# The samples' memory updates of an mLSTM layer in four row tiles, with selection products to lay out their rows, and one accumulator shared between the weight stream and the mixers

## The chip, the cores and the metric

One Trainium2 chip; the program runs on one core. The metric is the device time of one launch in microseconds, the median of several runs.

## The reference

Two layers run over 288 tokens: 256 of a prompt and 8 samples of 4 tokens. Layer 0 has an S5 and a GLA mixer, layer 1 an mLSTM with 4 heads of width 512; each layer ends in an MLP with squared ReLU. For this case the mLSTM's update of the samples' memories matters. Each of 8 samples has for each of 4 heads a memory of 512x512 that is read against q, decayed, given the products of its 4 tokens, and returned:

```python
num = jnp.einsum('bhts,bhse->bhte', sc, vc) + wp[..., None] * jnp.einsum('bhtd,bhde->bhte', qc, cm)
...
c_new = decay[..., None, None] * cm + jnp.einsum('bhs,bhsd,bhse->bhde', wk, kc, vc)
```

All of it is float32.

## The kernel before

**The stream.** Almost all work is products of the 288 tokens with weight matrices. `gemm` cuts a matrix into groups of 256 output columns, and each group into granules of 4 k-tiles. For a granule, SyncE loads the weights (`raw`), ScalarE rounds them to `wh` and VectorE forms the rest `wl` (`cast`, L187 and L188), and `mm` issues 2 x 4 x 3 = 24 matmuls of 128x128 by 288 columns (L202 to L204) into the group's two accumulators, PSUM tiles named `g` of the pool `psg`, which has 3 buffers. The group's last granule is followed by the evacuation of the two accumulators, mostly on VectorE. In layer 1 a group of the input projections has 4 granules, one of the output product 2.

**The side work.** The mixers are generators. After each granule `run` casts weights for a later granule and then lets every active generator advance (`pump`); a rate says how many steps it takes per granule. So the program's order on each engine is fixed when it is built: 24 stream matmuls, then whatever the generators issue in that step, then the next 24. TensorE works through this in order. PSUM has 8 banks: `psg` 3, `pss` 3 (tiles `s`, for nearly all side work), `psn` 2 (tiles `n`). The tiles of a pool are given out in turn, and a new tile waits until the last reader of the tile that held its buffer is done.

**The mLSTM.** `ml_head` prepares a head: the products of the prompt and the rows of k and v for the samples. A sample's k and v are split into a rounded part and a rest, and the four combinations stand in 128 rows (`ks0`, `vs`). `ml_mem` updates the memories. They come in 64 tiles `cin` of two samples (128x2x512) by GpSimd's DMA queue, 6 buffers. The function `masked` makes, once for four tiles, stationary operands `km` with all rows but one sample's set to zero. A step (rate 0.64) takes one tile; every second step first reads two tiles against q in four column tiles of 32 columns (L1545, tiles `n`):

```python
for b in range(2):
    pb = self.pss.tile([128, 512], F32, name="s")
    nc.tensor.matmul(pb, lhsT=km[:, 2 * i + b, :], rhs=vs, start=True, stop=True)
    c = 4 * (2 * i + b) + 3
    v.scalar_tensor_tensor(out=t[:, b, :], in0=t[:, b, :], scalar=wp[:, c:c + 1], in1=pb, ...)
```

So a sample's update is one product of 128 rows (L1551) into an `s` tile and one VectorE operation on 128x512 (L1553), 128 of each. `ml_gates` runs at the start of layer 1; its products with the gate weights `wg` (L1279) need a load that stands on GpSimd's queue (L1262 to L1270).

Of the kernel before, what the change touches and what calls it, by code (L numbers as in the profile page):

```python
# [23 lines left out]
R_S5, R_GLA, R_ML, R_MEM = (1.0, 1.2, 1.15), 1.0, 1.0, 0.64  # L24
R_GST, R_DEC, N_U = 0.5, 0.6, 2

# layout of the constants' array: name -> (first column, columns)
_CONST = {}
_at = 0
for _n, _w in (("ident", 128), ("par", 4), ("gmask", 128), ("gmask_s", 32), ("tri", 128), ("tri_s", 32),  # L30
               ("bm", 8), ("own", 2), ("sel", 32), ("selg", 8), ("selp", 32), ("sels", 32)):
    _CONST[_n] = (_at, _w)
    _at += _w
NCONST = _at


def const_array():
# [24 lines left out]
    sels = np.zeros((32, 32))  # L62
    sels[:, :8] = t32[:, None] // 4 == np.arange(8)[None, :]
    put("sels", sels)
    return c
# [11 lines left out]
class Base:  # L77
    def __init__(self, ctx, tc, I, O):
# [8 lines left out]
        self.psg = pool("psg", 3, space=PSUM)  # L87
        self.pss = pool("pss", 3, space=PSUM)
        self.psn = pool("psn", 2, space=PSUM)
        self.items, self.side, self.later, self.flags = [], [], [], set()  # L90
        m = self.main
# [99 lines left out]

    def mm(self, gr):
# [3 lines left out]
        if opens:  # L196
            g.ps = [self.psg.tile([128, T], F32, name="g") for _ in range(g.nm)]
# [91 lines left out]
    def rows_T(self, dst, src_rows, n):  # L289
        """dst[128, n] = the transposed rows of length 128 (n at most 128)."""  # L290
        ps = self.pss.tile([128, 512], F32, name="s")
        self.nc.tensor.transpose(ps[:, 0:n], src_rows, self.ident[0:n, 0:n])
        self.nc.vector.tensor_copy(out=dst, in_=ps[:, 0:n])

    def setup(self):
        nc, I, c = self.nc, self.I, self.const
        self.cst = c.tile([128, NCONST], F32, name="cst")
        nc.scalar.dma_start(out=self.cst, in_=I["consts"])
# [7 lines left out]
        # vectors, as columns; those of the first norm ahead of the rest  # L306
# [20 lines left out]
    def x_parts(self):  # L327
        """x for the first layer's input projections: it comes in quarters of its columns, each ahead of a granule."""
# [39 lines left out]
    def spread_r(self):  # L368
        """The tokens' scales, on all partitions."""
# [19 lines left out]
    def load_h(self):  # L389
        """x again, transposed, as the residual stream."""  # L390
# [15 lines left out]
NJ = 32          # pairs of groups  # L406
NCH = 72         # chunks: 8 of the samples, then 64 of the prompt
# [8 lines left out]
class S5:  # L416
# [59 lines left out]
    def s5_loads2(self, i):  # L476
        """More of the loads; they are spread over the first products."""
# [18 lines left out]
    def s5_tables(self):  # L496
# [7 lines left out]
        # A-bar: the states of a pair of groups on the partitions  # L504
# [51 lines left out]
        # (A-bar - 1) / a  # L556
# [15 lines left out]
        # A^8  # L572
# [5 lines left out]
        # C, block-diagonal and transposed, its imaginary part negated; B-bar  # L578
# [20 lines left out]
        # initial states of the samples  # L599
# [18 lines left out]
        def powers(q):  # L618
            """A^(3-s) B-bar of 4 pairs, block-diagonal."""
# [15 lines left out]
        def turn(q):  # L635
            """Their transposes, and the kernel between the tokens of a chunk (transposed)."""
# [17 lines left out]
        def adds(q):  # L654
            """What the chunks add to the states; the kernel."""
# [49 lines left out]
    def pairs(self, q, src, dst, n, t1, t2):  # L705
        """Every second of n chunks takes over the state that the chunk before it leaves (4 pairs of groups)."""
# [12 lines left out]
    def s5_scan(self):  # L719
# [8 lines left out]
        def last():  # L728
            """The samples' final states."""
# [22 lines left out]
    def s5_y(self):  # L752
# [15 lines left out]
        def table(q):  # L768
            """C A^(t+1) of 4 pairs, block-diagonal."""
# [54 lines left out]
        # y, split for the product with the gate's weights  # L824
# [9 lines left out]
        # final states  # L834
# [30 lines left out]
class GLA:  # L865
# [98 lines left out]
        # decays for q and k: within a chunk of the prompt they count from its middle  # L964
# [43 lines left out]
    def gla_head(self, h):  # L1008
# [6 lines left out]
        # scores within the chunks, and k decayed to the end of its chunk with the tokens on the partitions  # L1015
# [23 lines left out]
        # chunk states of the prompt  # L1039
# [15 lines left out]
        # states of the samples against q  # L1055
# [13 lines left out]
        # output  # L1069
# [19 lines left out]
    def gla_states(self):  # L1089
        """New states of the samples."""  # L1090
# [141 lines left out]
CB = 6           # buffers for the memories of two samples  # L1232
TE = TP + 40     # gate rows: the prompt, then each sample with a place for its state ahead of its tokens


class Layer1:
    def ml_open(self):
# [7 lines left out]
        self.kw1 = p.tile([128, 3, 512], F32, name="kw1")  # L1245
        self.hn, self.so, self.smp = {}, {}, {}
        self.yy = {}
        self.rb4 = p.tile([4, 608], F32, name="rb4")
# [5 lines left out]
        self.rbk = p.tile([128, T], F32, name="rbk")  # L1254

    def ml_gates(self):
# [3 lines left out]
        p = pc.__enter__()  # L1260
        wg = p.tile([128, ND, 32], F32, name="wg")
# [47 lines left out]
        # log-forget gates, their sums, the running maximum  # L1309
# [7 lines left out]
        a, b, wk = ff[:, 0:T], self.rb4[:, 0:T], fe[:, 0:T]  # L1317
        em, wp = self.rb4[:, T:2 * T], self.rb4[:, 2 * T:2 * T + NS]
# [17 lines left out]
        nc.gpsimd.dma_start(out=self.rb_dram, in_=self.rb4)  # L1336
# [52 lines left out]
    def ml_head(self, h):  # L1389
        nc, I, O = self.nc, self.I, self.O  # L1390
        v, act = nc.vector, nc.scalar
        q, k, vt, kw = self.q1, self.k1, self.vt1, self.kw1
# [13 lines left out]
        # decays between the tokens, transposed: source tokens on the partitions  # L1406
# [17 lines left out]
        # k with the tokens on the partitions, decayed to the end  # L1424
        for i, n in enumerate((128, 128, 32)):
# [3 lines left out]
            act.activation(out=kw[0:n, i, :], in_=ps[0:n].rearrange("p a b -> p (a b)"), func=AF.Copy,  # L1429
# [23 lines left out]
        for i, (n, c) in enumerate(((128, "selp"), (128, "selp"), (32, "sels"))):  # L1453
            for d in range(4):
                nc.tensor.matmul(ps[32 * d:32 * d + 32, :], lhsT=self.c(c)[0:n], rhs=kw[0:n, i, d * 128:d * 128 + 128],
# [9 lines left out]
        for r in (0, 64):  # L1465
            act.activation(out=vs[r:r + 32], in_=vt[0:32, 2, :], func=AF.Copy)
        for r in (32, 96):
            v.tensor_tensor(out=vs[r:r + 32], in0=vt[0:32, 2, :], in1=vs[0:32].bitcast(F32), op=ALU.subtract)
        # denominators
# [10 lines left out]
        yield  # L1480
        self.flags.add(f"vs{h}")
        yield
        # numerators, without the samples' memories
# [11 lines left out]
        # the prompt's memory  # L1495
# [12 lines left out]
    def ml_mem(self):  # L1508
# [16 lines left out]
        def masked(h, d):  # L1525
            km = p.tile([128, 8, 128], F32R, name="km")
            ks = self.smp[h]["k"][:, d * 128:d * 128 + 128].bitcast(F32)
            v.tensor_tensor(out=km, op=ALU.mult, in0=ks.rearrange("p (o c) -> p o c", o=1).to_broadcast([128, 8, 128]),
                            in1=self.c("bm").rearrange("p (b o) -> p b o", o=1).to_broadcast([128, 8, 128]))
            return km  # L1530

        for g in range(CB):
            load(g)
        for h in range(4):
            yield from self.until(f"vs{h}")
            s = self.smp[h]
            qp, wp, vs, rec = s["qp"], s["wp"], s["v"], s["rec"]
            km = masked(h, 0)
            yield
            pn = [self.psn.tile([128, 512], F32, name="n") for _ in range(2)]  # L1540
            for n in range(16):
                d, i = divmod(n, 4)
                if i % 2 == 0:
                    for b in range(4):
                        nc.tensor.matmul(pn[i // 2][32 * b:32 * b + 32, :], lhsT=qp[:, d, :],  # L1545
                                         rhs=cin[16 * h + n + b // 2][:, b % 2, :], start=d == 0, stop=d == 3)
                g = 16 * h + n
                t = cin.pop(g)
                for b in range(2):
                    pb = self.pss.tile([128, 512], F32, name="s")  # L1550
# [319 lines left out]
```

## Time and profile before

| | |
|---|---|
| three runs | 2812.74, 2813.13, 2815.81 us; median 2813.13 us |
| profiled execution, span from first to last instruction | 2813.8 us |
| TensorE, matmuls busy | 2778.5 us (99%) |
| VectorE busy | 1728.4 us (61%) |
| ScalarE busy | 1344.3 us (48%) |
| stretch with memory updates | 1423 to 1908 us of the span |

The span lies 0.7 us above the median of the runs; the profile gives no other time for that execution. A matmul's duration in the trace (some 0.3 us for the stream's) runs from its start to a modelled end, and matmuls overlap. What a matmul costs the stream is therefore the distance from its start to the next one's start; in the text this is called its pace.

### The profile page before, as it was taken

Reading aid. Unit: us, or ns where it says so; the run is one execution under the profiler, and the core shown is the slowest. Engines: PE = TensorE matmul, PEld = TensorE weight load, DVE = VectorE, ACT = ScalarE, POOL = GpSimd, SP = SyncE. Lnnn points to the kernel's source line nnn. Section 1 sums busy time; section 2 is a strip of 40 time slices with the busy share of each in tenths; the row PEclk is TensorE's granted clock in tenths of the full one; section 3 lists DMA queues with packets and bytes.
Section 4 is the critical chain, followed back from the end, with each engine's and each line's share of the span. In section 5 each row is a group of like instructions: output and inputs, shape, how many; then the busy total and the mean of one; then the engine's idle time right before and its main releaser. Section 6 shows DMA issues by size and latency. Waiting matters only on the chain.

```text
span 2813.8 us, 52593 instructions
## 1 busy us (share of the span) xinstructions
PE 2778.5 (99%) x20648; PEld 2688.8 (96%) x20648; DVE 1728.4 (61%) x3259; ACT 1344.3 (48%) x2459; POOL 212.3 (8%) x326
## 2 busy tenths in 40 slices
PE   8999999999999999999999999999999999999998
PEld 7988999999999999999988898889999999999998
DVE  7887668555555555556466665867655555555555
ACT  5646755544444444445433343445544444444445
POOL 3110112000000000000112222210000000000000
PEclk9999999999999999999999999999999999999999
DMA  7455567555555555555678878875555555555554
GB/s 210 130 155 140 161 195 228 160 167 165 165 164 165 163 168 164 166 164 146 197 223 250 269 249 271 266 254 173 164 166 164 166 165 165 164 167 163 167 165 131
DMA packets 449511, 511.86 MB, mean 182 GB/s; under 512 B 23282, under 2 KB 423052, under 8 KB 449232
## 3 DMA queue, kind: packets, MB, share of 16 engines
q1 hardware_dynamic: 414320, 412.67, 48.6%
q0 software_dynamic: 28096, 90.16, 10.1%
q10 hardware_dynamic: 6848, 5.68, 0.6%
q8 instruction: 162, 2.65, 0.4%
q14 instruction: 85, 0.70, 0.1%
HBM read 460.08 MB, written 47.56 MB: 180 GB/s over the span
## 4 chain that ended last, share of the span: by engine, by line
PE 94%; DVE 4%; ACT 1%; issue 1%; DMA 0%; ACTq 0%; DVEq 0%
PE g L202 29%; PE g L203 28%; PE g L204 28%; PE s L1551 1%; PE n L1545 1%; PE s L1500 1%; DVE wl L188 1%; PE n L801 1%; PE s L664 0%; PE s L1419 0%; ACT wh L187 0%; DVE hr L745 0%; PE n L798 0%; PE s L1490 0%; PE s L643 0%
## 5 line engine op out<-in xcount | busy, mean ns | idle before, releaser
L187 ACT ACTIVATE wh<-raw 128x512 fp32r<-128x512 f32 x1556 | 963.1, 629 | 1203.0 <-PE g L203 1153.7
L188 DVE TENSOR_TENSOR wl<-raw,wh 128x512 fp32r<-128x512 f32 x1556 | 1035.8, 688 | 664.3 <-ACT wh L187 652.2
L202 PE MATMUL g<-xh,wh 128*128 128x288 f32 x3856 | 1158.6, 300 | 3.0 <-DVE gy L938 1.4
L204 PE MATMUL g<-xh,wl 128*128 128x288 f32 x3856 | 1138.2, 295 | 3.8 <-DVE wl L188 3.7
L203 PE MATMUL g<-xl,wh 128*128 128x288 f32 x3856 | 1141.0, 296 | 0.0
L202 PEld LDWEIGHTS g<-xh,wh 128*128 128x128 f32 x3856 | 726.4, 188 | 14.4 <-issue 9.5
L204 PEld LDWEIGHTS g<-xh,wl 128*128 128x128 f32 x3856 | 728.9, 189 | 5.4 <-DVE wl L188 5.4
L203 PEld LDWEIGHTS g<-xl,wh 128*128 128x128 f32 x3856 | 727.4, 189 | 5.2 <-issue 3.3
L203 PE MATMUL g<-hl,wh 128*128 128x288 f32 x2048 | 606.2, 296 | 0.0
L204 PE MATMUL g<-hh,wl 128*128 128x288 f32 x2048 | 605.2, 296 | 0.0
L202 PE MATMUL g<-hh,wh 128*128 128x288 f32 x2048 | 604.7, 295 | 0.0
L202 PEld LDWEIGHTS g<-hh,wh 128*128 128x128 f32 x2048 | 389.1, 190 | 0.0
L204 PEld LDWEIGHTS g<-hh,wl 128*128 128x128 f32 x2048 | 384.0, 188 | 0.0
L203 PEld LDWEIGHTS g<-hl,wh 128*128 128x128 f32 x2048 | 383.8, 187 | 0.0
L1727 DVE TENSOR_TENSOR hr<-hr,g 128x288 f32<-128x288 f32 x256 | 116.3, 454 | 186.6 <-PE g L204 186.6
L1719 ACT ACTIVATE us<-sq 128x288 f32<-128x288 f32 x128 | 56.9, 445 | 146.2 <-DVE sq L1718 146.2
L1718 DVE SCALAR_TENSOR_TENSOR sq<-g,rbc 128x288 f32<-128x288 f32 x128 | 58.5, 458 | 94.5 <-PE g L204 94.3
L1553 DVE SCALAR_TENSOR_TENSOR cin<-cin,wps,s 128x512 f32<-128x512 f32 x128 | 89.7, 742 | 7.4 <-PE s L1551 6.7
L1523 POOL DMA_DIRECT2D cin<-in_state_mlstm_c_dram x64 | 45.3, 708 | 305.6 <-DMA out_sample_mlstm_c_dram<-cin 284.0
L1334 POOL DMA_DIRECT2D out_sample_mlstm_m_dram<-mo x1 | 0.6, 620 | 838.7 <-DVE mk L1338 838.7
L1720 ACT ACTIVATE hh<-us 128x288 fp32r<-128x288 f32 x128 | 57.0, 445 | 4.1
L203 PE MATMUL g<-yl,wh 128*128 128x288 f32 x192 | 56.7, 295 | 0.0
(504 smaller groups left out, 1928.9 us busy)
## 6 DMA issues: line engine op xcount, KB each, us to landing
raw<-in_w_mlp_up_dram SPq DMA_DIRECT2D x256, 512.0 KB, 3.7
raw<-in_w_mlp_down_dram SPq DMA_DIRECT2D x256, 512.0 KB, 3.6
raw<-in_w_in_odd_dram SPq DMA_DIRECT2D x128, 512.0 KB, 4.6
raw<-in_w_in_even_dram SPq DMA_DIRECT2D x64, 512.0 KB, 4.0
cin<-in_state_mlstm_c_dram POOLq DMA_DIRECT2D x64, 512.0 KB, 5.2
out_sample_mlstm_c_dram<-cin POOLq DMA_DIRECT2D x64, 512.0 KB, 5.5
raw<-in_w_out_even_dram SPq DMA_DIRECT2D x32, 512.0 KB, 4.4
raw<-in_w_out_odd_dram SPq DMA_DIRECT2D x32, 512.0 KB, 3.6
```

Source lines behind the costliest of these rows:

```text
L187: nc.scalar.activation(out=wh[:, 0:n], in_=src, func=AF.Copy)
L188: nc.vector.tensor_tensor(out=wl[:, 0:n], in0=src, in1=wh[:, 0:n].bitcast(F32), op=ALU.subtract)
L202: nc.tensor.matmul(g.ps[j], lhsT=wh, rhs=xh, start=opens and k == 0, stop=False)
L203: nc.tensor.matmul(g.ps[j], lhsT=wh, rhs=xl, start=False, stop=False)
L204: nc.tensor.matmul(g.ps[j], lhsT=wl, rhs=xh, start=False, stop=closes and k == n - 1)
L801: nc.tensor.matmul(ps[:, j, :], lhsT=t3[:, ri, j].rearrange("p t c -> p (t c)"), rhs=eh[:, ri, jj, 0:NCH], start=False, stop=ri == 1)
L1523: nc.gpsimd.dma_start(out=cin[g], in_=part(I["state_mlstm_c"], g))
L1553: v.scalar_tensor_tensor(out=t[:, b, :], in0=t[:, b, :], scalar=wp[:, c:c + 1], in1=pb, op0=ALU.mult, op1=ALU.add)
L1718: nc.vector.scalar_tensor_tensor(out=t, in0=ps, scalar=0.0, in1=self.rbc, op0=ALU.max, op1=ALU.mult)
L1719: nc.scalar.activation(out=sq, in_=t, func=AF.Square)
L1720: nc.scalar.activation(out=hh[:, j, :], in_=sq, func=AF.Copy)
L1727: nc.vector.tensor_add(out=self.h[:, j, :], in0=self.h[:, j, :], in1=ps)
```

## The change

The 128 updates are regrouped. A step takes two tiles, that is four samples, at half the rate (0.32), so that 32 steps do what 64 did. The four samples' rows stand in four groups of 32 partitions, and the four products contract over 32 rows each, one in each row tile of the array. Each writes an own PSUM bank, so a step needs four tiles at a time. One of them, `x`, comes from a new pool `psx` with a single buffer; three are `s`. The rows are laid out by a product with a 0/1 matrix `rsel` (L1473 and the like, twice a head, 64 rows by 128 columns by 512) and copied out by ScalarE; `masked` and the vector work that wrote the rows before go. The pool `psg` has 2 buffers now. Outside the mLSTM's mixer every third accumulator of the stream comes from `psx`, so that the stream has three as before; from the opening of layer 1 until its second output product (`three` is False) it has two.

```diff
+        self.psg = pool("psg", 2, space=PSUM)
+        self.psx = pool("psx", 1, space=PSUM)
...
+    def gtile(self):
+
+        self.gat += self.three
+        if self.three and self.gat % 3 == 0:
+            return self.psx.tile([128, 512], F32, name="x")[:, 0:T]
+        return self.psg.tile([128, T], F32, name="g")
...
-            g.ps = [self.psg.tile([128, T], F32, name="g") for _ in range(g.nm)]
+            g.ps = [self.gtile() for _ in range(g.nm)]
...
+        self.rsel = p.tile([64, 2, 128], F32R, name="rsel")
+        self.nc.gpsimd.dma_start(out=self.rsel, in_=self.I["consts"][0:64, NCST:NCST + 256].rearrange("p (a c) -> p a c", a=2))
+        self.three = False
...
-        ks0 = s["k"] = p.tile([128, 512], F32R, name="ks0", bufs=2)
-        for r in (0, 32):
-            act.activation(out=ks0[r:r + 32], in_=kw[0:32, 2, :], func=AF.Copy)
-        for r in (64, 96):
-            v.tensor_tensor(out=ks0[r:r + 32], in0=kw[0:32, 2, :], in1=ks0[0:32].bitcast(F32), op=ALU.subtract)
+        ks = s["k"] = p.tile([128, 2, 512], F32R, name="ks", bufs=2)
+        hl = p.tile([64, 512], F32R, name="hl")
+        act.activation(out=hl[32:64], in_=kws, func=AF.Copy)
+        v.tensor_tensor(out=hl[0:32], in0=kws, in1=hl[32:64].bitcast(F32), op=ALU.subtract)
         yield
+        ps = self.pss.tile([128, 512], F32, name="s")
+        nc.tensor.matmul(ps, lhsT=self.rsel[:, 0, :], rhs=hl, start=True, stop=True)
+        for a in range(2):
+            act.activation(out=ks[:, a], in_=ps, func=AF.Copy, scale=self.c("par")[:, a:a + 1])
...
+        ps = self.pss.tile([128, 512], F32, name="s")
+        nc.tensor.matmul(ps, lhsT=self.rsel[:, 1, :], rhs=hl, start=True, stop=True)
+        act.activation(out=vs, in_=ps, func=AF.Copy)
...
+            for n in range(8):
+
+                d, a = divmod(n, 2)
+                ds = slice(d * 128, d * 128 + 128)
+                g = 16 * h + 2 * n
+                t = [cin.pop(g + i) for i in range(2)]
+                for b in range(4):
+                    nc.tensor.matmul(pn[a][32 * b:32 * b + 32, :], lhsT=qp[:, d, :], rhs=t[b // 2][:, b % 2, :],
+                                     start=d == 0, stop=d == 3)
+                pb = [self.psx.tile([128, 512], F32, name="x")] + [self.pss.tile([128, 512], F32, name="s") for _ in range(3)]
+                for b in range(4):
+                    rs = slice(32 * b, 32 * b + 32)
+                    nc.tensor.matmul(pb[b], lhsT=ks[rs, a, ds], rhs=vs[rs], start=True, stop=True)
+                for b in range(4):
+                    o = t[b // 2][:, b % 2, :]
+                    c = 4 * (4 * a + b) + 3
+                    v.scalar_tensor_tensor(out=o, in0=o, scalar=wp[:, c:c + 1], in1=pb[b], op0=ALU.mult, op1=ALU.add)
+                    if b % 2:
+                        nc.gpsimd.dma_start(out=part(O["sample_mlstm_c"], g + b // 2), in_=t[b // 2])
+                        load(g + b // 2 + CB)
...
+            if h:
+                self.need("mem3")
+                self.call(lambda: setattr(self, "three", True))
```

The first place is on TensorE, in the second head, where a step of `ml_mem` meets steps of two other generators behind the same granule: `facc,ones` is the norm of the first head's output, `vt,kw` the prompt's memory. Before:

```order
L204 MATMUL g<-xh,wl 128x288
L1545 MATMUL n<-cin,qp 32x512 x4
L1551 MATMUL s<-vs,km 128x512 x2
L1597 MATMUL s<-facc,ones 128x288
L1500 MATMUL s<-vt_15503,kw_15504 128x512 x2
L202 MATMUL g<-xh,wh 128x288
```

And after, at the same place:

```order
L223 MATMUL g<-xh,wl 128x288
L1566 MATMUL n<-cin,qp 32x512 x4
L1571 MATMUL x<-vs,ks 128x512
L1571 MATMUL s<-vs,ks 128x512 x3
L1617 MATMUL s<-facc,ones 128x288
L1527 MATMUL s<-vt_15506,kw_15507 128x512 x2
L221 MATMUL g<-xh,wh 128x288
```

A step now writes all three `s` tiles, where it wrote two, before another generator asks for one.

The second place is VectorE's order there: `q` is an evacuation of the stream's accumulators, `wl` the casts, `facc` the norm. Before:

```order
L1359 TENSOR_TENSOR q_15501<-g,rbc 128x288 x2
L188 TENSOR_TENSOR wl<-raw,wh 128x512 x2
L1553 SCALAR_TENSOR_TENSOR cin<-cin,wps,s 128x512 x2
L272 RECIPROCAL facc<-sq 128x288
L188 TENSOR_TENSOR wl<-raw,wh 128x512 x2
```

And after:

```order
L1382 TENSOR_TENSOR q_15504<-g,rbc 128x288 x2
L200 TENSOR_TENSOR wl<-raw,wh 128x512 x2
L1575 SCALAR_TENSOR_TENSOR cin<-cin,wps,x 128x512
L1575 SCALAR_TENSOR_TENSOR cin<-cin,wps,s 128x512 x3
L291 RECIPROCAL facc<-sq 128x288
L200 TENSOR_TENSOR wl<-raw,wh 128x512 x2
```

Two operations on the memories in a row have become four; the first is that on the `x` tile.

The third place is GpSimd's queue ahead of layer 1. Before:

```order
L1127 DMA out_sample_gla_dram<-s_5685 128x2x256
L1262 MEMSET wg 128x512
L1263 DMA wg<-in_w_in_odd_dram 128x16x8
L1265 DMA bi<-in_mlstm_b_i_dram 4x1
L1266 DMA bi<-in_mlstm_b_f_dram 4x1
```

And after:

```order
L1146 DMA out_sample_gla_dram<-s_5688 128x2x256
L1275 DMA rsel<-in_consts_dram 64x256
L1285 MEMSET wg 128x512
L1286 DMA wg<-in_w_in_odd_dram 128x16x8
L1288 DMA bi<-in_mlstm_b_i_dram 4x1
```

The load of `rsel`, into memory that the first MLP uses until its last product, now stands ahead of the gate weights' load.

## Rows read from the trace of the kernel before

**Rows 1.** The page: busy time, share and instructions by engine; clock by slices.

```profile
PE 2778.5 (99%) x20648; PEld 2688.8 (96%) x20648; DVE 1728.4 (61%) x3259; ACT 1344.3 (48%) x2459; POOL 212.3 (8%) x326
...
PEclk9999999999999999999999999999999999999999
```

**Rows 2.** The page: the chain that ended last, by engine.

```profile
PE 94%; DVE 4%; ACT 1%; issue 1%; DMA 0%; ACTq 0%; DVEq 0%
```

**Rows 3.** Busy time by stretches around layer 1's mixer.

```profile
core 0: us, PE busy (x) PEld busy (x) DVE busy (x) ACT busy (x) POOL busy (x), PEclk, DMA share, GB/s
...
1423.00:1908.00 485.00, 482.53 (x3362) 419.87 (x3355) 321.03 (x522) 193.21 (x338) 107.35 (x164) 1.00 0.82 258
1908.00:1960.00 52.00, 52.00 (x394) 51.90 (x393) 41.29 (x78) 30.04 (x56) 0.42 (x1) 1.00 0.55 169
```

**Rows 4.** TensorE who waits for whom, 1423 to 1908 us: total, times, longest.

```profile
PE s L1500 <- DVE cin L1553: 1.7, 2, 1.5
PE g L202 <- DVE so L1384: 0.3, 1, 0.3
```

**Rows 5.** Timeline of TensorE, updates without reads: start, length, operation, count.

```profile
1458.49 0.29 PE L204 MATMUL g<-xh,wl 128*128 128x288 f32 x1
1458.62 0.63 PE L1551 MATMUL s<-vs,km 128*128 128x512 f32 x2
1459.09 0.29 PE L202 MATMUL g<-xh,wh 128*128 128x288 f32 x1
1459.22 0.29 PE L203 MATMUL g<-xl,wh 128*128 128x288 f32 x1
```

**Rows 6.** Timeline of TensorE, updates behind reads.

```profile
1508.12 1.06 PE L1545 MATMUL n<-cin,qp 128*32 128x512 f32 x8
1509.11 0.73 PE L1551 MATMUL s<-vs,km 128*128 128x512 f32 x2
1509.67 0.29 PE L202 MATMUL g<-xh,wh 128*128 128x288 f32 x1
```

**Rows 7.** Timeline of TensorE, updates behind transposes of v.

```profile
1489.40 1.10 PE L1551 MATMUL s<-vs,km 128*128 128x512 f32 x2
1490.42 0.66 PE L1428 MATMUL s<-cst,k 128*128 128x128 f32 x4
```

**Rows 8.** The chain in order of time: start, us, what.

```profile
1432.19 1.72 PE s L1500 x4
...
1438.81 1.00 PE n L1545 x8
```

**Rows 9.** Timeline of VectorE around 1509 us.

```profile
1507.98 1.28 DVE L188 TENSOR_TENSOR wl<-raw,wh 128x512 fp32r<-128x512 f32 x2
1509.65 1.41 DVE L1553 SCALAR_TENSOR_TENSOR cin<-cin,wps,s 128x512 f32<-128x512 f32 x2 [0.38 <-PE s L1551]
```

**Rows 10.** Timeline of TensorE and VectorE where two generators follow the updates.

```profile
1562.74 0.73 PE L1551 MATMUL s<-vs,km 128*128 128x512 f32 x2
1563.32 0.65 PE L1597 MATMUL s<-facc,ones 128*128 128x288 f32 x2
1563.43 1.40 DVE L1553 SCALAR_TENSOR_TENSOR cin<-cin,wps,s 128x512 f32<-128x512 f32 x2
...
1564.23 1.12 PE L1500 MATMUL s<-vt,kw 128*128 128x512 f32 x2 [0.26 <-DVE cin L1553]
```

**Rows 11.** The same on TensorE, in the last head.

```profile
1847.95 0.65 PE L1597 MATMUL s<-facc,ones 128*128 128x288 f32 x2
1850.05 1.13 PE L1500 MATMUL s<-vt,kw 128*128 128x512 f32 x2 [1.46 <-DVE cin L1553]
```

**Rows 12.** VectorE's groups, 1423 to 1908 us: busy, mean ns, idle before.

```profile
L188 DVE TENSOR_TENSOR wl<-raw,wh 128x512 fp32r<-128x512 f32 x212 | 142.4, 688 | 118.6 <-ACT wh L187 114.8 <-PE s L1372 3.6
L1553 DVE SCALAR_TENSOR_TENSOR cin<-cin,wps,s 128x512 f32<-128x512 f32 x128 | 89.7, 742 | 7.4 <-PE s L1551 6.7
L1528 DVE TENSOR_TENSOR km<-ks,cst 128x1024 fp32r<-128x1024 f32 x15 | 18.3, 1217 | 0.0
L1479 DVE RECIPROCAL rec<-rec 128x288 f32<-128x288 f32 x3 | 5.9, 1953 | 0.1
L1362 DVE TENSOR_TENSOR k<-g,rbk 128x288 f32<-128x288 f32 x12 | 5.5, 455 | 6.3 <-PE g L204 6.2
```

**Rows 13.** The gate weights' load, timeline of GpSimd's queue.

```profile
488.86 0.52 POOL L1262 MEMSET wg<- 128x512 f32 x1 [2.57 <-PE g L204]
489.68 1.18 POOL L1263 DMA_DIRECT2D wg<-in_w_in_odd_dram  x1 [0.29 <-POOL wg L1262]
```

**Rows 14.** The same load, its landing.

```profile
DMA to landing us min/median/max: 5.5/5.5/5.5
```

**Rows 15.** TensorE at the end of the first MLP and at the gates.

```profile
1301.18 0.30 PE L204 MATMUL g<-hh,wl 128*128 128x288 f32 x1
1301.32 0.29 PE L202 MATMUL g<-xh,wh 128*128 128x288 f32 x1
...
1311.48 0.45 PE L1279 MATMUL s<-xh,wg 128*32 128x288 f32 x4
```

More of the change, by code (lines that the diff above doesn't have):

```diff
@@ L23 @@
 NEG = -1e30
-R_S5, R_GLA, R_ML, R_MEM = (1.0, 1.2, 1.15), 1.0, 1.0, 0.64
+R_S5, R_GLA, R_ML, R_MEM = (1.0, 1.2, 1.15), 1.0, 1.0, 0.32
 R_GST, R_DEC, N_U = 0.5, 0.6, 2
@@ L30 @@
 for _n, _w in (("ident", 128), ("par", 4), ("gmask", 128), ("gmask_s", 32), ("tri", 128), ("tri_s", 32),
-               ("bm", 8), ("own", 2), ("sel", 32), ("selg", 8), ("selp", 32), ("sels", 32)):
+               ("bm", 8), ("own", 2), ("sel", 32), ("selg", 8), ("selp", 32), ("sels", 32),
+               ("rk", 128), ("rv", 128)):
     _CONST[_n] = (_at, _w)
@@ L34 @@
 NCONST = _at
+NCST = _CONST["rk"][0]
 def const_array():
@@ L61, in const_array @@
     put("selp", selp)
-    sels = np.zeros((32, 32))
-    sels[:, :8] = t32[:, None] // 4 == np.arange(8)[None, :]
+    sels = np.zeros((64, 32))
+    sels[32:, :8] = t32[:, None] // 4 == np.arange(8)[None, :]
     put("sels", sels)
+    g, p, a, t = r // 32, r // 16 % 2, r // 4 % 4, r % 4
+    tok = 4 * (g + 4 * p) + t
+    src = np.arange(64)[:, None]
+    put("rk", src == tok + 32 * (1 - a // 2))
+    put("rv", src == tok + 32 * (a % 2))
     return c
@@ L86, in __init__ @@
         self.tmp = pool("tmp", 2)
-        self.psg = pool("psg", 3, space=PSUM)
+        self.psg = pool("psg", 2, space=PSUM)
+        self.psx = pool("psx", 1, space=PSUM)
         self.pss = pool("pss", 3, space=PSUM)
@@ L90, in __init__ @@
         self.items, self.side, self.later, self.flags = [], [], [], set()
+        self.three, self.gat = True, 0
         m = self.main
@@ L296, in setup @@
         nc, I, c = self.nc, self.I, self.const
-        self.cst = c.tile([128, NCONST], F32, name="cst")
-        nc.scalar.dma_start(out=self.cst, in_=I["consts"])
+        self.cst = c.tile([128, NCST], F32, name="cst")
+        nc.scalar.dma_start(out=self.cst, in_=I["consts"][:, 0:NCST])
         self.ident = self.c("ident")
@@ L1244, in ml_open @@
         self.vt1 = p.tile([128, 3, 512], F32, name="vt1")
-        self.kw1 = p.tile([128, 3, 512], F32, name="kw1")
+        self.kw1 = p.tile([128, 2, 512], F32, name="kw1")
+        self.kws1 = self.vt1[32:64, 2, :]
         self.hn, self.so, self.smp = {}, {}, {}
         self.yy = {}
-        self.rb4 = p.tile([4, 608], F32, name="rb4")
         self.aT = p.tile([128, 3, 4], F32, name="aT")
@@ L1260, in ml_gates @@
         p = pc.__enter__()
+        rb4 = p.tile([4, 608], F32, name="rb4")
         wg = p.tile([128, ND, 32], F32, name="wg")
@@ L1316, in ml_gates @@
         yield
-        a, b, wk = ff[:, 0:T], self.rb4[:, 0:T], fe[:, 0:T]
-        em, wp = self.rb4[:, T:2 * T], self.rb4[:, 2 * T:2 * T + NS]
+        a, b, wk = ff[:, 0:T], rb4[:, 0:T], fe[:, 0:T]
+        em, wp = rb4[:, T:2 * T], rb4[:, 2 * T:2 * T + NS]
         v.tensor_sub(out=a[:, 0:TP], in0=ie[:, 0:TP], in1=F[:, 0:TP])
@@ L1335, in ml_gates @@
         nc.gpsimd.dma_start(out=O["prompt_mlstm_m"][0, 0].rearrange("(h o) -> h o", o=1), in_=mo[:, 8:9])
-        nc.gpsimd.dma_start(out=self.rb_dram, in_=self.rb4)
+        nc.gpsimd.dma_start(out=self.rb_dram, in_=rb4)
         dc = mk[:, 0:128]
@@ L1391, in ml_head @@
         v, act = nc.vector, nc.scalar
-        q, k, vt, kw = self.q1, self.k1, self.vt1, self.kw1
+        q, k, vt, kw, kws = self.q1, self.k1, self.vt1, self.kw1, self.kws1
         yield from self.until("gates")
@@ L1464, in ml_head @@
         vs = s["v"] = p.tile([128, 512], F32R, name="vs", bufs=2)
[L1465 to L1468, printed above, removed]
+        act.activation(out=hl[0:32], in_=vt[0:32, 2, :], func=AF.Copy)
+        v.tensor_tensor(out=hl[32:64], in0=vt[0:32, 2, :], in1=hl[0:32].bitcast(F32), op=ALU.subtract)
         ps = self.pss.tile([128, T], F32, name="s")
@@ L1480, in ml_head @@
         yield
+        ps = self.pss.tile([128, 512], F32, name="s")
+        nc.tensor.matmul(ps, lhsT=self.rsel[:, 1, :], rhs=hl, start=True, stop=True)
+        act.activation(out=vs, in_=ps, func=AF.Copy)
+        yield
         self.flags.add(f"vs{h}")
-        yield
         if h >= 2:
@@ L1523, in load @@
                 nc.gpsimd.dma_start(out=cin[g], in_=part(I["state_mlstm_c"], g))
[L1525 to L1530, printed above, removed]
         for g in range(CB):
@@ L1536, in ml_mem @@
             s = self.smp[h]
-            qp, wp, vs, rec = s["qp"], s["wp"], s["v"], s["rec"]
-            km = masked(h, 0)
-            yield
+            qp, wp, ks, vs = s["qp"], s["wp"], s["k"], s["v"]
             pn = [self.psn.tile([128, 512], F32, name="n") for _ in range(2)]
[L1541 to L1550, printed above, removed]
-                    nc.tensor.matmul(pb, lhsT=km[:, 2 * i + b, :], rhs=vs, start=True, stop=True)
-                    c = 4 * (2 * i + b) + 3
-                    v.scalar_tensor_tensor(out=t[:, b, :], in0=t[:, b, :], scalar=wp[:, c:c + 1], in1=pb,
-                                           op0=ALU.mult, op1=ALU.add)
-                nc.gpsimd.dma_start(out=part(O["sample_mlstm_c"], g), in_=t)
-                load(g + CB)
-                if i == 3 and d < 3:
-                    km = masked(h, d + 1)
-                if n < 15:
@@ new lines, in ml_mem @@
+            for n in range(8):
[17 more added lines that the diff above has]
+                        load(g + b // 2 + CB)
+                if n < 7:
```

6 lines of the change are left out of this document (3 added, 3 removed).

## The prediction

> **What bounds the kernel now.** I read the page first. TensorE is busy for 99% of the span at nearly the full clock, VectorE for 61%, ScalarE for 48% [rows 1], and the chain that ended last is 94% TensorE [rows 2]. In the stretch with the memory updates TensorE is busy 482.5 of 485 us, VectorE 321.0, the DMA engines 82% [rows 3]. The list of waits in that stretch shows TensorE waiting for other engines three times, 2.0 us in all [rows 4]. So the time is the sum of what TensorE is given in its fixed order, plus what it waits, and I count both. The timelines give prices: the reader should look at the distance between starts, not at the lengths. The stream steps by 0.13 us, and a pair of updates without reads holds it up by 1459.09 - 1458.62 = 0.47 us [rows 5], a pair behind reads by 0.56 [rows 6].
>
> **What goes from TensorE.** Of the 64 pairs 32 stand without reads and 32 behind them: 32 x 0.47 + 32 x 0.56 = 33.0 us. Five pairs, three of them like the one in [rows 7], take 0.4 to 0.55 us more (1.02 against 0.47), because the second product waits for an `s` tile that the transposes of v hold: 2.5 us. Last, there are two places where the third `s` tile goes to the norm (`facc,ones`) and the prompt's memory then waits for the first update's tile. At the first TensorE would have gone on at about 1563.8, half a microsecond behind the norm's start, and went on at 1564.23 [rows 10]; at the second the wait is 1.6 us beyond that half [rows 11]: 2.0 us together. Sum: 37.5 us.
>
> **What four row tiles cost.** No product of the trace runs in row tiles, but the reads run in column tiles: eight instructions of 512 columns, two rounds of four, start to end in 1.00 us, while the same kind over the full array steps by 1.72 / 4 = 0.43 us each [rows 8], that is 3.4 us for eight. Column tiles do run at the same time, and the block costs 0.13 us beyond its two rounds, which I put down to the changes of the array's shape. The nearest price for a block of updates is then: one product's pace 0.23, its first weight load uncovered behind the reads 0.10 (0.56 against 0.47), the change of shape 0.13: 0.46 us, times 32: 14.7. From below: no extra change of shape, 0.33, 4.2 us less. From above: nothing runs at the same time, 4 x 0.23 + 0.23 = 1.15 us, 22 us more. I take 0.46, because the reads are the same kind of thing turned by a quarter. The eight selection products are single ones with a change of shape each: 0.46 x 8 = 3.7.
>
> For the pace of row tiles the Trainium skill has a figure ("TensorE: Matmul & The Clock Gate", Part 3, Measured speedup vs the span model): four row tiles with 512 columns 3.07 times as fast. By it a block would cost 4 x 0.23 / 3.07 = 0.31 us, an estimate, and the sum would be 5 us lower; no run here has shown row tiles yet.
>
> **What the wider block makes wait.** This is the term that decides. A step now takes `x` and all three `s` tiles. The next `s` tile is the one of the block's second product, and VectorE frees it with its second operation. In the trace the second operation ends at 1509.65 + 1.41 = 1511.06, 1.95 us after the first product started [rows 6, 9]; TensorE starts 0.06 us behind such an end (1563.43 + 0.74 = 1564.17, then 1564.23) [rows 10, 12]. So whoever asks for an `s` tile right behind a block starts 2.0 us after the block's start instead of 0.46: a wait of 1.55 us, in which the stream stands still, because it is queued behind. In the program's order after the change this happens behind 16 of the 32 blocks: 4 times the prompt's memory, 3 numerators, 3 transposes of k, 2 denominators, 2 selection products, 2 norms (one of them is the first place in the section on the change); behind the other 16 comes the stream, and one granule of 3.2 us lets VectorE finish. 16 x 1.55 = 24.8 us. Before, the third tile was free at all but the two places above. The bounds: 1.95 us is nearly the least of the trace, since VectorE was idle just before [rows 9]; where it still has casts the second operation ends later, up to 0.8 us more (two casts of 0.69 ahead) [rows 12].
>
> The rule for it is in the Trainium skill, "TensorEngine Tiling (Array Packing)", PSUM Bottleneck and Gotcha 1: row tiles write different PSUM banks, and once the products are four times as fast their evacuation may be the limit. The trace agrees in its parts: 0.66 us from one memory operation to the next (1.41 for two of 0.74) against 0.46 for the whole block.
>
> **Two accumulators.** With two `g` tiles a group's first granule waits for the evacuation of the group before, where the third tile gave it 1.6 us more. The evacuation stands on VectorE behind the memory operations of the step before: four end at 0.54 + 0.74 + 3 x 0.66 = 3.3 us behind the block's start, the evacuation of 0.455 [rows 12] at 3.7; TensorE is through with block and granule at 3.7. So alone a block costs 0.0 to 0.2 us; with a reciprocal (1.95) or other work of the heads ahead it costs 0.4 to 1.0. In the order I count five groups of the first kind and eight of the second among the 40 that open in this state: 4 us, at least 0, at most 8. If VectorE had no such burst, this would cost nothing: the first evacuation is done half a granule ahead.
>
> **What is hidden.** VectorE loses `masked` (16 x 1.2) and four short operations a head, some 25 us; it bounds no stretch, so nothing comes back, as its waits in [rows 4] are counted already. ScalarE's twelve copies of 128x512 replace eight small ones. Rate and loads of the memories stay: two tiles at half the rate. The load of `rsel` now waits on GpSimd's queue for the last product of the first MLP, at about 1301.5 [rows 15], and the gate weights behind it: with 0.6 us for `rsel`'s issue, memset and issue at the distances of [rows 13], 5.5 us to landing [rows 14], they land at about 1308.6. The gates' products start at 1311.48 [rows 15], so 2.9 us are left; what the load takes beyond that is paid in full.
>
> **Sum.** 14.7 + 3.7 + 24.8 + 4 - 37.5 = +9.7 us. The profiled span of 2813.8 becomes 2823.5, the median of 2813.1 becomes **2823 us**, 0.35% slower. (A measurement of this kernel tells a change from none at about 0.2%, 5.6 us.) Its own range, from 0.33 us a block and free accumulators to VectorE later by 0.3 us at 16 places and accumulators at 8 us: 2815 to 2832.
>
> **Rivals.**
> First, on the other side: the waits for `s` tiles do not bind, and what the array saves stays: 37.5 - 14.7 - 3.7 - 4 = 15.1 us, 2798. It decides when the mean wait falls under 15.1 / 16 = 0.94 us, so VectorE's second operation would have to end 1.4 us after the block's start instead of 1.95. For it: VectorE is idle for a third of the stretch [rows 3]. Against it: two operations of 0.74 us are in that 1.95, and it was measured with VectorE idle. Chance 0.12.
> Second, the change does not do what it says: row tiles of this data type run one after the other, or load their weights so. 22 us more, 2845, and somewhat less if only the loads are in turn. Against it: the column tiles of [rows 8]. Chance 0.08.
> Third, the terms meet: the blocks are cheaper than I put them (0.33), the accumulators free, and some waits covered by others; within 5.6 us of before, some 2815. Chance 0.18.
> My forecast has 0.62. Slower than by 0.2% are forecast and second rival, 0.70; within it the third, 0.18; faster the first, 0.12. As the cases have both signs, the range reaches from between the first and the third, 2805, to a little beyond the forecast's own, 2835; some 0.1 lies below and 0.07 above.
>
> **What the profile after would show.** Right: the four products of a block start within some 0.01 us of each other, and the stream follows 0.4 to 0.5 us behind the first; the list of waits names TensorE waiting for the memory operation some 16 times, about 1.5 us each, at the lines of the heads; VectorE's `km` is gone; the stretch of updates is some 10 us longer although TensorE's busy time in it falls. Wrong: those waits under 0.9 us or at fewer places (the sign turns), products of a block 0.23 us apart (row tiles in turn), a wait at the opening products of the stream for its evacuations of more than 8 us in all, or a gap before the gates' products at about 1311 us.

## The result, and the profile after

The changed kernel took 2843.09 us (median of four runs, 2840.36 to 2847.19) against 2814.31 (2812.74 to 2815.81) for the kernel before in the same comparison: 1.0103 times as long, 95% interval 1.0091 to 1.0115. That is 28.8 us more, where 9.7 were forecast: the sign was right, the size was not, and the time lies above the range.

The profiled execution has a span of 2838.6 us, 24.8 more than before. The page of it, engines and clock by slices, against [rows 1]:

```profile
PE 2775.5 (98%) x20656; PEld 2681.8 (94%) x20656; DVE 1706.6 (60%) x3235; ACT 1346.7 (47%) x2463; POOL 212.8 (7%) x327
...
PEclk9999999999999999999999999999999999999999
```

TensorE is busy 3 us less in a span that is 25 us longer, so it stands, or runs slower while it is called busy. The timelines say where. TensorE comes to the gates and to the norm behind layer 1's mixer at (after, then the norm before):

```profile
1311.11 0.69 PE L1302 MATMUL s<-xh,wg 128*32 128x288 f32 x8
...
2013.57 0.65 PE L297 MATMUL s<-sacc,ones 128*128 128x288 f32 x2
```

```profile
1989.32 0.65 PE L278 MATMUL s<-sacc,ones 128*128 128x288 f32 x2
```

From the gates to this norm it is 702.5 us, and 677.8 before (from 1311.48, [rows 15]). The difference, 24.6, is all but 0.2 of the profiled one, so only this layer's mixer is told of below. The gates' products begin 0.57 us behind the last norm's: the late load of `wg` is hidden, as forecast. The same window as [rows 3]:

```profile
core 0: us, PE busy (x) PEld busy (x) DVE busy (x) ACT busy (x) POOL busy (x), PEclk, DMA share, GB/s
1423.00:1908.00 485.00, 457.68 (x3218) 393.98 (x3218) 286.66 (x477) 187.41 (x330) 102.47 (x157) 0.98 0.79 247
```

27.3 us without a matmul where there were 2.5, and a granted clock of 0.98 instead of 1.00. The list of TensorE's waits over the span (waited for, total us, times, longest) says for whom, against [rows 4]:

```profile
...
PE s L1527 <- DVE cin L1575: 6.5, 4, 2.0
PE s L1517 <- DVE cin L1575: 4.8, 3, 1.6
PE s L1451 <- DVE cin L1575: 4.6, 3, 1.6
PE s L1473 <- DVE cin L1575: 3.9, 2, 2.0
...
PE s L1617 <- DVE cin L1575: 3.3, 2, 1.6
PE s L1496 <- DVE cin L1575: 3.0, 2, 1.5
...
PE g L221 <- DVE hr L1695: 1.3, 2, 1.1
...
PE g L221 <- DVE q L1382: 1.0, 1, 1.0
```

The first six lines are the 16 places of the prediction, 26.1 us in all. One of them on TensorE's timeline (start, length, operation), and what follows it:

```profile
1500.49 1.07 PE L1566 MATMUL n<-cin,qp 128*32 128x512 f32 x8
1501.48 0.50 PE L1571 MATMUL x<-vs,ks 32*128 32x512 f32 x1
1501.49 0.51 PE L1571 MATMUL s<-vs,ks 32*128 32x512 f32 x3
1503.95 0.46 PE L1473 MATMUL s<-hl,rsel 64*128 64x512 f32 x1 [1.96 <-DVE cin L1575]
...
1505.44 0.46 PE L221 MATMUL g<-xh,wh 128*128 128x288 f32 x1
1505.70 0.44 PE L222 MATMUL g<-xl,wh 128*128 128x288 f32 x1
1505.94 0.44 PE L223 MATMUL g<-xh,wl 128*128 128x288 f32 x1
...
1508.82 0.41 PE L223 MATMUL g<-xh,wl 128*128 128x288 f32 x1
1509.06 0.30 PE L221 MATMUL g<-xh,wh 128*128 128x288 f32 x1
1509.20 0.29 PE L222 MATMUL g<-xl,wh 128*128 128x288 f32 x1
```

The block's four products start within 0.01 us. The `s` request behind them waits 1.96 us. Then the stream steps by 0.24 us from 1505.7 to 1508.8, and by 0.13 again from 1509.1. The windows of that place (PE busy, granted clock, DMA share, GB/s) give the reason:

```profile
1495.00:1505.60 10.60, 8.54 (x80) 1.00 0.85 250
1505.60:1509.00 3.40, 3.40 (x15) 0.51 0.83 281
1509.00:1515.00 6.00, 6.00 (x48) 1.00 0.41 114
```

For 3.4 us TensorE ran at half its clock, 1.2 instead of 2.4 GHz, and it counts as wholly busy there. The mixer has six such stretches after the change (from 1505.6, 1693.4, 1771.9, 1788.9, 1847.0 and 1949.4 us); five begin 1.2 to 2 us behind the end of one of the 16 waits, the sixth 1.6 us behind a wait of 1.3 us for a cast, which the kernel before does not have. Behind the other 11 of the 16 waits no stretch follows. Before, the mixer had one, at 1332.7 among the gates. The page's row of slices cannot show them: a slice is 71 us.

Where no `s` request follows, the stream stands behind the block (TensorE's timeline, then a group's opening for which an accumulator is late):

```profile
1584.66 0.50 PE L1571 MATMUL x<-vs,ks 32*128 32x512 f32 x1
1584.67 0.50 PE L1571 MATMUL s<-vs,ks 32*128 32x512 f32 x3
1585.10 0.40 PE L221 MATMUL g<-xh,wh 128*128 128x288 f32 x1
1585.33 0.30 PE L222 MATMUL g<-xl,wh 128*128 128x288 f32 x1
...
1589.54 0.37 PE L221 MATMUL g<-xh,wh 128*128 128x288 f32 x1 [0.99 <-DVE q L1382]
```

The stream follows after 0.44 us, and its first product then takes 0.23 instead of 0.13.

### The profile page after: what moved, and what is told of

It is laid out like the page before. It is cut to its first block, busy times and chain, and to the rows that moved or that the text cites. A ratio compares the mean times of both kernels' runs of the same rounds, so it can differ in the third digit from the quotient of the medians.

```text
span 2838.6 us, 52604 instructions
## 1 busy us (share of the span) xinstructions
PE 2775.5 (98%) x20656; PEld 2681.8 (94%) x20656; DVE 1706.6 (60%) x3235; ACT 1346.7 (47%) x2463; POOL 212.8 (7%) x327
## 5 line engine op out<-in xcount | busy, mean ns | idle before, releaser
L221 PE MATMUL g<-xh,wh 128*128 128x288 f32 x2936 | 889.8, 303 | 3.7 <-DVE gy L957 1.4
L222 PE MATMUL g<-xl,wh 128*128 128x288 f32 x2936 | 871.9, 297 | 0.0
L223 PE MATMUL g<-xh,wl 128*128 128x288 f32 x2936 | 869.3, 296 | 1.7 <-DVE wl L200 1.7
L222 PE MATMUL g<-hl,wh 128*128 128x288 f32 x1352 | 400.2, 296 | 0.0
L223 PE MATMUL g<-hh,wl 128*128 128x288 f32 x1352 | 399.5, 296 | 0.0
L221 PE MATMUL x<-xh,wh 128*128 128x288 f32 x920 | 274.5, 298 | 0.0
L223 PE MATMUL x<-xh,wl 128*128 128x288 f32 x920 | 271.6, 295 | 1.1 <-DVE wl L200 1.1
L222 PE MATMUL x<-xl,wh 128*128 128x288 f32 x920 | 272.3, 296 | 0.0
L222 PE MATMUL x<-hl,wh 128*128 128x288 f32 x696 | 206.0, 296 | 0.0
L223 PE MATMUL x<-hh,wl 128*128 128x288 f32 x696 | 205.7, 296 | 0.0
```

What stands on the lines that cost most here:

```text
L221: nc.tensor.matmul(g.ps[j], lhsT=wh, rhs=xh, start=opens and k == 0, stop=False)
L222: nc.tensor.matmul(g.ps[j], lhsT=wh, rhs=xl, start=False, stop=False)
L223: nc.tensor.matmul(g.ps[j], lhsT=wl, rhs=xh, start=False, stop=closes and k == n - 1)
```

## The experiments

Two theories stood after the result. Mine: the 16 waits cost what was forecast; what is missing is the half clock that they bring, and something on the two accumulators. The rival: the clock is incidental, and the shared accumulator costs far more than the 4 us I gave it. Every time below is a median, with its ratio to the kernel before in the same comparison and a 95% interval (the kernel before took 2814.13 us beside the first four runs and 2814.73 beside the last four). The ratio goes by the means of the runs, so it can differ by some 0.0005 from that of the medians.

**The memory's step last in its gap.** With no other `s` request behind a block, no wait is left; the four products and the two accumulators stay.

```diff
-R_S5, R_GLA, R_ML, R_MEM = (1.0, 1.2, 1.15), 1.0, 1.0, 0.32
+R_S5, R_GLA, R_ML, R_MEM = (1.0, 1.2, 1.15), 1.0, 1.0, 0.31
...
-        for s in list(self.side):
+        for s in sorted(self.side, key=lambda s: "mem0" in s[3]):
```

> The changed kernel, with the memory step emitted last among the generators of a granule (and its rate 0.31 for 0.32, so that the last head's output finds its buffers). Behind each of the 32 blocks then stands the stream, none of the 16 requests for an s tile. My theory (16 waits of 1.7 us, 27 us in all, and half-clock windows that these waits bring on, some 10 to 12 us): both go, 2803 to 2808 us, no TensorE wait for the memory operation, and no or one half-clock window between 1400 and 2000 us. Rival A (the waits alone, the half-clock windows come by chance): 2814 to 2818, windows as many as now (six). Rival B (the two accumulators are what the sum lacked): waits go, but 10 us and more of waits at group openings stay, 2816.

2811.10 us, ratio 0.9994 (0.9985 to 1.0003): 32 us less than the changed kernel, as long as before, and 3 us above the 2808 that I expected at most. The waits for the memory operations are gone from the list; what is left at the block, 4.3 us that I had not counted, is for tiles that ScalarE still empties:

```profile
PE s L1571 <- ACT cp L1529: 1.8, 2, 1.4
PE s L1571 <- ACT vs L1507: 1.3, 1, 1.3
...
PE s L1571 <- ACT sq L290: 1.2, 1, 1.2
```

The mixer has one stretch at half clock instead of six, and it begins 0.5 us behind one of these waits, of 1.4 us. So the order of requests carries nearly the whole loss, the clock's part with it. What that order is worth without row tiles, the control below tells.

**The lent tile last in the block.** The next free `s` tile then comes with VectorE's first operation, not its second.

```diff
-pb = [self.psx.tile([128, 512], F32, name="x")] + [self.pss.tile([128, 512], F32, name="s") for _ in range(3)]
+pb = [self.pss.tile([128, 512], F32, name="s") for _ in range(3)] + [self.psx.tile([128, 512], F32, name="x")]
```

> The changed kernel with the x tile as the last of the four products in place of the first, so that VectorE's first operation of a block frees the next s tile, and not its second. Theory: each of the 16 waits falls by one step of VectorE, 0.66 us, to about 1.0 us, 10.6 us in all, and with shorter waits some of the half-clock windows go: 2826 to 2833 us. Rival A (the windows come by chance): 2832 to 2834. A rival by which the waits are not what costs: 2843, unchanged.

2830.64 us, ratio 1.0058 (1.0046 to 1.0071). The same 16 places wait 17.6 us instead of 26.1, and two stretches at half clock are left of six. The mixer is 14.0 us shorter: 8.5 of wait, and four stretches of some 1.5 us each (next run) make 14.5.

**Products in place of waiting.** Six products with zero weights, added to the accumulator of the reads, ahead of the `s` request at 14 of the 16 places.

```diff
...
+        if self.hot:
+            z, vs, pn = self.hot
+            for _ in range(NFILL):
+                self.base.nc.tensor.matmul(pn, lhsT=z, rhs=vs, start=False, stop=False)
+            self.hot = None
+        return self.p.tile(*a, **k)
...
+NFILL = 6
...
```

> The changed kernel with six products of a zero operand, added to the accumulator of the memory reads (which leaves it as it is), ahead of the request for an s tile behind 14 of the 16 blocks. TensorE works there for 1.3 us where it waited; the end of the wait is set by VectorE as before. Theory: the waits' time stays but TensorE is not idle, so the half-clock windows go: 8 to 12 us faster than the changed kernel, 2831 to 2835, with no or one window between 1400 and 2000 us. Rival A (windows by chance): 2843 to 2846, six windows.

2835.34 us, ratio 1.0076 (1.0063 to 1.0089): 7.8 us less than the changed kernel, with intervals that do not meet, for 84 products more. The timeline and the mixer's window (columns as in [rows 3]):

```profile
1490.46 0.50 PE L1590 MATMUL s<-vs,ks 32*128 32x512 f32 x3
1490.89 1.66 PE L95 MATMUL n<-vs,zero 128*128 128x512 f32 x6
1492.45 0.66 PE L1470 MATMUL s<-cst,k 128*128 128x128 f32 x4
```

```profile
1413.00:1914.00 501.00, 494.59 (x3467) 421.32 (x3466) 300.75 (x499) 195.15 (x342) 106.02 (x162) 1.00 0.79 249
```

Waits of 26 us became 24 us of products and 5 of waits; the next user starts as far behind its block, 2.0 us here. But the granted clock is 1.00, two stretches at half clock are left, and the time fell. Neither of the two stands behind a block: one begins at 1333.4 us among the gates, as in the kernel before, the other at 1944.4 behind the wait of 1.3 us for a cast, like the sixth of the changed kernel. The mean clock of the five runs is 0.994 to 0.996, that of the changed kernel's four runs 0.992 to 0.994. A stretch holds 3.4 / 0.24 = 14 stream products that lose 0.107 us each, 1.5 us; four fewer are 6 us, and the mixer became 5.4 us shorter. That the idle waits behind the blocks bring the half clock is shown. Why 5 of the 16 were followed by it and the others were not is open.

**Two accumulators in the kernel before.** The mixer of layer 1 gets two, nothing else.

```diff
...
+            return self.psx.tile([128, 512], F32, name="x")[:, 0:T]
+        return self.psg.tile([128, T], F32, name="g")
...
+        self.three = False
...
```

> The kernel before with the accumulators alone changed: two of the stream in the mLSTM's mixer, three elsewhere, the x tile used by the stream only. Theory: 2 to 5 us slower, 2816 to 2819, no new half-clock windows. Rival B (two accumulators are what the sum lacked): 12 us and more, 2826 to 2830.

2823.25 us, ratio 1.0034 (1.0022 to 1.0046): 9.1 us, more than I expected, less than the rival. TensorE waits 6.4 us at the openings of groups, in eight places; one of them, of 1.9 us, is followed by a stretch at half clock, which I had not expected. The 6.4 of waits and 1.5 for the stretch make 7.9 of the 9.5 us by which its mixer is longer.

**The order alone, in the kernel before.** The control for the first run.

```diff
-        for s in list(self.side):
+        for s in sorted(self.side, key=lambda s: "mem0" in s[3]):
```

> The kernel before with the memory's step emitted behind all other side work of the same gap, nothing else: a control for the run with the changed kernel's memory last. My account (row tiles and selection products save some 19 us of TensorE's own work, two accumulators give 3 to 9 of it back): the order alone takes away the 2.0 us of waits at the norm and some of the 2.5 us at the transposes, and adds up to 3 us where an update asks for an `s` tile that ScalarE is still emptying, so 2810 to 2815, about as long as before. Rival (the order was what the earlier run gained from, and row tiles are worth nothing once their wait is gone): 2806 or less, below the changed kernel with memory last (2811).

2808.16 us, ratio 0.9981 (0.9972 to 0.9990): faster than both kernels, and between the two expectations. Besides the two waits, the order saves costly resumptions of the stream, that is, starts of the stream behind side work of another kind. The timeline, with the prompt's memory (`vt,kw`) followed by an update pair, and by the stream:

```profile
1546.08 1.88 PE L1500 MATMUL s<-vt,kw 128*128 128x512 f32 x4
1547.89 1.07 PE L1545 MATMUL n<-cin,qp 128*32 128x512 f32 x8
1548.88 0.73 PE L1551 MATMUL s<-vs,km 128*128 128x512 f32 x2
1549.45 0.30 PE L202 MATMUL g<-xh,wh 128*128 128x288 f32 x1
1549.58 0.29 PE L203 MATMUL g<-xl,wh 128*128 128x288 f32 x1
...
1552.64 1.88 PE L1500 MATMUL s<-vt,kw 128*128 128x512 f32 x4
1553.95 0.70 PE L202 MATMUL g<-xh,wh 128*128 128x288 f32 x1
1554.49 0.29 PE L203 MATMUL g<-xl,wh 128*128 128x288 f32 x1
```

Behind a pair the stream's second product follows the first by 0.13 us, behind the prompt's memory by 0.54. In this order a pair is the last thing in its gap 64 times, before 38 times; summed by starts over the mixer, the stream takes 519.6 us instead of 526.4. So the rival was half right: this order is worth 6.6 us by itself in the medians, and in it row tiles with all that comes with them show no gain (2811.10, with intervals that meet). Nor is a loss shown: in the profiled executions the mixer takes 670.7 us with them and 673.0 without.

**The order and two accumulators.**

> The run before this one and two accumulators in the second mixer. Two theories of what the third accumulator is worth. One (the price hangs on which of VectorE's operations stand ahead of a group's evacuation, so on where the memory's steps stand; in the changed kernel with memory last TensorE waited only 0.8 us more for `g` tiles): 2 to 5 us over the run before this one. The other (a fixed price of some 9 us, as in the kernel before with two accumulators): 8 to 11 us over it, and TensorE's waits for `g` tiles of 5 us or more.

2817.37 us, ratio 1.0012 (1.0003 to 1.0021): 9.2 us over the run before. My account fell: with the memory's operations behind the rest the price is what it was with them in between. At 1410.73 TensorE waits 1.01 us for the evacuation `q`, and VectorE's timeline shows what stands ahead of it:

```profile
1408.32 1.96 DVE L1488 RECIPROCAL rec<-rec 128x288 f32<-128x288 f32 x1
1410.19 0.76 DVE L1368 TENSOR_TENSOR q<-g,rbc 128x288 f32<-128x288 f32 x2
```

At this place it is the heads' own vector work. The other waits for `g` tiles, 4.9 of 5.9 us, are not followed here.

**Row tiles in twos, three accumulators kept.** The selection stays; a step updates two samples as two row tiles in two `s` tiles, memory last.

```diff
...
-                pb = [self.psx.tile([128, 512], F32, name="x")] + [self.pss.tile([128, 512], F32, name="s") for _ in range(3)]
-                for b in range(4):
-                    rs = slice(32 * b, 32 * b + 32)
+                pb = [self.pss.tile([128, 512], F32, name="s") for _ in range(2)]
+                for b in range(2):
+                    rs = slice(64 * r + 32 * b, 64 * r + 32 * b + 32)
...
```

> Row tiles without lending the third accumulator: the selection of the changed kernel, but two row tiles to a step, 64 steps as before, two `s` tiles each, three accumulators, memory last. My account (row tiles of a pair run at the same time and cost one product's pace with the change of shape, 0.33 behind the stream and 0.43 behind reads, where a pair now costs 0.47 and 0.56): 64 pairs save 8.6 us, the selection products cost 3.7, so some 5 us under the control with memory last. Rival (a pair's change of shape eats what the second tile saves, so a pair costs 0.45 or more): 2 to 4 us over the control.

2817.64 us, ratio 1.0012 (1.0003 to 1.0021): 9.5 over the control, further out than the rival. There is no half clock in its mixer to blame. A pair in its stream, on TensorE's timeline:

```profile
1453.91 0.29 PE L222 MATMUL g<-xh,wl 128*128 128x288 f32 x1
1454.14 0.50 PE L1571 MATMUL s<-vs,ks 32*128 32x512 f32 x2
1454.57 0.40 PE L220 MATMUL g<-xh,wh 128*128 128x288 f32 x1
1454.80 0.30 PE L221 MATMUL g<-xl,wh 128*128 128x288 f32 x1
```

From the stream's last product to its second one behind the pair it is 0.89 us, so the pair costs 0.89 - 2 x 0.13 = 0.63; by the same count the pair of [rows 5] costs 1459.22 - 1458.49 - 0.26 = 0.47. The two row tiles do run together, in 0.43 us, but the stream pays 0.10 ahead of them and 0.10 behind. Summed by starts over the mixer, against the control: the pairs take 28.0 us instead of 37.2, the stream 528.9 instead of 519.6, and the selection products 3.3 more. What the row tiles save, the stream gives back.

**Memory steps held back.** The changed kernel, memory last, and a step put off by up to one gap when another generator has just asked for an `s` tile.

```diff
...
+            if "mem0" in s[3] and self.pss.n != self.seen and s[2] < LATE:
+                s[2] += s[1] * part
+                continue
...
```

> The changed kernel with memory last, and a memory step held back by up to one gap where other side work has just asked for an `s` tile; the last head's split waits until the first output product is issued. Blocks right behind another user of `s` fall from 19 to 10 of 32, none has one behind it. My account (what memory last left of waits are the 4.3 us for tiles that ScalarE was still emptying): 2807 to 2810, with waits at the block of 2 us or less. Rival (those waits were covered by other work or come back at the accumulators): 2811 to 2814.

2814.67 us, ratio 1.0005 (0.9996 to 1.0013): my account fell. The waits at the block did not shrink, and the split that this version holds back is late itself (list of waits):

```profile
PE s L1587 <- ACT cp L1545: 4.2, 3, 2.7
PE g L236 <- ACT yh L1649: 2.9, 1, 2.9
```

Three stretches at half clock came with them.

## Why the prediction was right in sign and wrong in size

**Right.** The step said to decide did decide: 16 requests behind a block, forecast 24.8 us, listed 26.1. Row tiles run at the same time (second rival out), VectorE's `km` is gone, the selection products came to 3.6 us of pace (forecast 3.7), the load of `wg` is hidden, and the two accumulators cost the changed kernel 2.3 us of waits in the list above (`q` and `hr`), and some tenths at other openings (forecast 4, at most 8; no run of the changed kernel has three, so its price there is known by these waits alone). The first rival fell: the mean wait was 1.6 us, not under 0.94.

**Wrong: the sum had no term for TensorE's clock.** The prediction counts "what TensorE is given in its fixed order, plus what it waits" at the prices of a full clock. Six stretches at half clock instead of one cost 5 x 1.5 = 7.5 us; by the starts of the stream's products in those stretches it is 7.4. The filled run shows that the waits behind the blocks cause the five that follow them. The trace of the kernel before had a sign of it, which the prediction did not use: its one stretch begins 0.8 us behind a wait of 1.1 us among the gates, and the window ahead of those in [rows 3] (columns as there) shows a clock of 0.98:

```profile
1310.00:1423.00 113.00, 111.39 (x867) 105.34 (x866) 61.82 (x128) 50.52 (x93) 12.78 (x23) 0.98 0.57 167
```

The Trainium skill has this as a way to lose ("TensorE: Matmul & The Clock Gate", A second HAM failure mode: psum-queue depth-cycling): short idle times between groups of products, from cycling PSUM banks, let the clock swing between its levels. The trace agrees; that section gives no price by which the sum could have been mended, and the 1.5 us is of these runs.

**Mis-sized: "one product's pace 0.23, its first weight load uncovered 0.10, the change of shape 0.13: 0.46".** The block itself took 0.43 to 0.44. But the change of shape is paid at both ends, and the end behind the block, 0.10 us on the stream's next product, was not in it. At 16 blocks this is 1.7 us, at the selection products and others of their kind about 1. The trace of the kernel before had such ends too, behind products of 32 columns or of 32 rows:

```profile
1503.14 0.99 PE L1455 MATMUL s<-kw,cst 128*32 128x128 f32 x24
1504.07 0.40 PE L202 MATMUL g<-xh,wh 128*128 128x288 f32 x1
1504.31 0.29 PE L203 MATMUL g<-xl,wh 128*128 128x288 f32 x1
```

The stream's second product follows the first by 0.24 us. These side products are plain float32, so the kind changes there as well as the shape; that the shape alone does it, the runs with row tiles show. The prediction's "No product of the trace runs in row tiles" holds only in that none run side by side: 32 products `w,vt` and 8 `w,ones` of this mixer contract over 32 rows, all in the same row tile.

For the pace itself the Trainium skill's "TensorE: Matmul & The Clock Gate", Part 3, Measured speedup vs the span model, gives 3.07 for four row tiles. (The prediction's estimate from it, 4 x 0.23 / 3.07, is 0.30 us and not 0.31.) Here four in turn would be 4 x 0.23 = 0.92 us, so the block was 2.1 times as fast, and 1.7 times with the 0.10 behind it. The measurement decides.

**What the sum becomes.** 9.7 forecast; 7.4 for the clock; 2.7 at the ends of blocks and selections; 1.9 because blocks with their waits took 41.4 us from start to start instead of 39.5: 21.7 of the 24.6 us in the trace. Of the other 3 us, 1.6 are small changes in other side products next to blocks. The rest I do not place in full: the new wait of 1.3 us for a cast is in it, but the forecast also holds 4 us for accumulators, of which waits of 2.3 us were listed. The medians lie 4 us further apart. Of this, 2.7 us are there because the profiled execution was the fastest of the four; the others took 1.2 to 6.8 us more. Their mean clocks, 0.992 to 0.994, are not below its 0.992, so the clock does not explain that excess, and it stays open. The rest is that the kernel before was profiled in a slower execution than its median: some 2815.6 us, an estimate from its span and the 1.8 us by which each run of the changed kernel exceeds its span.

**The third accumulator** is worth 9 us in the kernel before, in two orders of the side work. In the changed kernel fewer openings met late evacuations. Why fewer stays open; the forecast of 4 lies near the waits of this kernel's order and is no general price.

## What to carry to other kernels

Before widening a block, look at who asks for the same buffers next in an in-order queue: here row tiles saved some 16 us of array time (36.1 of pairs less 13.8 of blocks, 3.6 of selections and 2.7 at their ends), lost 26 to the next request, and 7 more to the clock that followed. Price a short product of another shape by the stream's steps on both sides of it, not by its own pace. And try the free edit first: letting the memory's step go last in its gap gave 2808.16 us, less than either kernel, with no change to any product.

## What the runs showed of the hardware

TensorE waits of 1.5 to 2.0 us were followed by stretches at a granted clock of 0.5, which is 1.2 GHz, five times in 16, with the engine busy in them throughout. Waits of 1.1 us (gates) and 1.3 us (a cast) were followed by one as well, and a wait of 1.46 us in the kernel before [rows 11] was not, so these runs give no length of wait that decides. Filling such waits with products that add nothing gave back 7.8 us in the median, and no stretch stood behind a block any more. Row tiles of 32 rows and 512 columns started within 0.01 us of one another, and two took as long as four, 0.43 us; entering and leaving them cost the neighbours of the full array 0.10 us each.
